# RWKV-7 + FoX trunk on one core: value and bonus rows with the heads of a pair apart, the gate loaded for two chunks at once, the bias row put in order by ScalarE

## The chip, the cores and the metric

The kernel runs on one core of one Trainium2 chip. The metric is the device time of one execution in microseconds (us), lower is better; a kernel's time is the median of several runs.

## The reference

A two-layer decoder trunk in float32: 1024 tokens (T), width 1024 (D), 16 heads of 64. The change lies in the first mixer, RWKV-7 time mixing, of which this is the part that matters:

```python
r, k, v = x_r @ w_rkv[0], x_k @ w_rkv[1], x_v @ w_rkv[2]
g = sigmoid(x_g @ g1) @ g2
def step(S, inp):
    r_t, w_t, k_t, v_t, kk_t, b_t = inp
    sa = einsum('bhvk,bhk->bhv', S, -kk_t)
    S = S * w_t[:, :, None, :] + sa[..., None] * b_t[:, :, None, :] + v_t[..., None] * k_t[:, :, None, :]
    return S, einsum('bhvk,bhk->bhv', S, r_t)
_, y = lax.scan(step, S0, (r, w, k, v, kk, b))
y = group_norm(y) * lnx_w + lnx_b
bonus = sum(r_h * k_h * r_k, axis=-1, keepdims=True) * v_h
x = x + ((y + bonus) * g) @ w_o
```

After it come a squared-ReLU MLP, the shared keys and values, forgetting attention and a second MLP.

## The kernel before, in words

The scan is done in 16 chunks of 64 tokens (`C` = 64, `c` the chunk). The 16 heads are treated as 8 pairs (`NK` = 8, index `p`), `h` is the head within a pair; `P` is 128. Large products are done in float32 split into a high and a low part (`hi`, `lo`; `whi`, `wlo`), three products for one.

The stages, in the profiled run: projections of k and r to 281 us (L863), the projection of v from 281 to 376 us (`proj_tokens`, L884: 768 matmuls of 128x256), the gate's first product to 399 us, then the chunked recurrence, which overlaps the gate's second product at its start and is over by about 690 us, then the rest of the trunk.

**Values.** `emit_v` takes a finished 256-token, 256-column block of v from PSUM (ScalarE copies it to `tv`, L1059), makes the bonus times v in `vb` (ScalarE at L1065 for the first two column blocks, VectorE at L1067 for the others), adds the bias row `lnb` on VectorE (L1071), and writes `vb` to the DRAM array `d_vb` on SyncE's queue (L1072) and `tv` to `d_v` on ScalarE's queue (L1073). Both arrays have the tokens as rows and the columns in the order of the model (pair, head, value). `bon` holds the bonus factor for each token and head (L1033). `lnb` is loaded by one broadcast DMA (L1055).

**Recurrence.** For each chunk `rec_values` loads `Z`, the values of a chunk (L400): for each head of a pair 64 tokens x 8 pairs x 64 values, that is 512 pieces of 256 bytes. `rec_norm` loads `Vh` from `d_vb` in the same way (L543), and `rec_gate_load` loads 128x8x64 of the gate array `d_g` (L563, 1024 pieces of 256 bytes). The chain of one chunk on TensorE is `pp` (AE times Z; ScalarE copies it to `Ps`, L493), `yp`, `sa` (from Ps; VectorE writes Z, L505), `u` (from Z; VectorE writes the next Z, L519), `yp`. `prepare` for the next chunk lies between (`ap`, `tp`, `op`; results `AE` and `BKt`, `TT` copied by ScalarE at L482). GpSimd scales the state `St` (L524), `KRz` (L471) and the block `B` (L435). The tiles of d_T and d_B that a chunk needs are loaded as `TT`, `BT` and `B`.

**Fill.** W_out's products (`wo`) are put between the steps of a chunk to fill TensorE. Their weights come in pieces: SyncE loads `woraw` (L1200), ScalarE casts it to `woh` (L597), and VectorE (L600) or GpSimd (L602) makes the low part `wol`. The gate's second product `gp` fills the first chunks; ScalarE copies it out (L1265: `xt`, `gs`) and writes `d_g` on its own queue (L1267).

**What sets the order.** A scheduler orders the instructions of each engine from a simulated timeline, except where the program order is pinned; a change in one place therefore moves instructions elsewhere. A queue (SyncE's or ScalarE's) issues its DMAs strictly in this order, and each DMA that these two queues issue takes one of eight completion semaphores in turn, so that it waits for the DMA issued eight places before.

Of the kernel before, what the change touches and what calls it, by code (L numbers as in the profile page):

```python
# [390 lines left out]
LANES = [(slice(0, 32), slice(32, 64)), (slice(64, 96), slice(96, 128))]  # L391


def rec_values(k, c):

    nc = k.nc
    Z = k.rc.tile([P, NK, 2, C], F32, tag="Z", name="Z", bufs=2)
    v = k.d_v[c * C:c * C + C, :].rearrange("t (p h v) -> h t p v", h=2, v=C)
    for h in range(2):
        nc.sync.dma_start(Z[HALF[1 - h], :, h], v[h])  # L400
        if c == 0:
            nc.gpsimd.memset(Z[HALF[h], :, h], 0.0)
    return Z


# [78 lines left out]

def rec_solve(k, s, Z):

    nc, c = k.nc, s["c"]
    pp = k.psC.tile([P, NK, C], F32, tag="psC", name="pp")
    for p in range(NK):
        for h, hs in enumerate(HALF):  # L490
            k.pe.matmul(pp[hs, p], s["AE"][:, p, h, 0, :], Z[:, p, h, :], start=True, stop=True)
    Ps = k.rw.tile([P, NK, C], F32, tag="Ps", name="Ps")
    nc.scalar.copy(Ps, pp)  # L493
    yp = s["yp"] = k.psY.tile([P, NK, C], F32, tag="psY", name="yp")
    if c:
        for p in range(NK):
            for h, hs in enumerate(HALF):
                k.pe.matmul(yp[hs, p], s["KR"][hs, p, 1, :], Z[hs, p, h, :], start=p == 0, stop=False)
    yield
    sa = k.psC.tile([P, NK, C], F32, tag="psC", name="sa")  # L500
    for p in range(NK):
        for h, hs in enumerate(HALF):
            k.pe.matmul(sa[hs, p], s["TT"][:, p, h, :], Ps[:, p], start=True, stop=True)
    for h, hs in enumerate(HALF):
        nc.vector.tensor_tensor(Z[hs, :, h], sa[hs], k.ns2[hs, :, c:c + 1].broadcast_to([64, NK, C]), op=ALU.mult)  # L505


def rec_state(k, s, Z, Zn, St):

    nc, c = k.nc, s["c"]  # L510
    u = k.psC.tile([P, NK, C], F32, tag="psC", name="u")
    for p in range(NK):
        for h, hs in enumerate(HALF):
            k.pe.matmul(u[hs, p], s["BKt"][:, p, hs], Z[:, p, h, :], start=True, stop=True)
    for h, hs in enumerate(HALF):
        if St is None:
            nc.vector.tensor_copy(Zn[hs, :, h], u[hs])
        else:
            nc.vector.tensor_tensor(Zn[hs, :, h], u[hs], St[hs], op=ALU.add)  # L519
    if c == NCH - 2:  # L520
        return None
    Sn = k.rw.tile([P, NK, C], F32, tag="St", name="St")
    for h, hs in enumerate(HALF):
        nc.gpsimd.tensor_tensor(Sn[hs], Zn[hs, :, h], k.sc[hs, :, c:c + 1].broadcast_to([64, NK, C]), op=ALU.mult)  # L524
    return Sn


def rec_out(k, s, Z):
    c = s["c"]
    for p in range(NK):  # L530
        for h, hs in enumerate(HALF):
            k.pe.matmul(s["yp"][hs, p], s["AE"][:, p, h, 1, :], Z[:, p, h, :], start=c == 0 and p == 0,
                        stop=p == NK - 1)


def rec_norm(k, s):

    nc, w, w1, c = k.nc, k.rw, k.rw1, s["c"]
    S3 = [P, NK, C]
    cs = slice(c * C, c * C + C)  # L540
    V = w1.tile(S3, F32, tag="Vh", name="Vh")
# [12 lines left out]
    rsqrt_small(k, w, rs, var, 1.0 / C, 64e-5)
    nc.vector.tensor_tensor(Y, Y, rs.unsqueeze(2).broadcast_to(S3), op=ALU.mult)
    nc.gpsimd.tensor_tensor(Y, Y, k.lnw, op=ALU.mult)
    nc.gpsimd.tensor_tensor(Y, Y, V, op=ALU.add)


def rec_gate_load(k, s):  # L560
    c = s["c"]
    s["g"] = k.rw.tile([P, NK, C], F32, tag="g", name="g")
    k.nc.sync.dma_start(s["g"], k.d_g.rearrange("(p f) t -> f p t", f=P)[:, :, c * C:c * C + C])  # L563
# [14 lines left out]
def stage_recurrence(k, a, tile_of, gates):  # L578
    nc, tc = k.nc, k.tc
    with ExitStack() as ctx:  # L580
# [107 lines left out]
        for c in range(NCH):  # L688
# [179 lines left out]

def proj_tokens(k, bank, xs, w, emit, lo_eng):

    wv = w.rearrange("(k p) e -> p k e", p=P)
    G, B = w.shape[1] // 256, T // 256
    for g in range(G):
        with k.tc.high_priority(offset=PRIO):
            pcs = [load_w(k, wv[:, 4 * q:4 * q + 4, 256 * g:256 * g + 256], [P, 4, 256], lo_eng=lo_eng) for q in range(2)]
        os_ = [bank().rearrange("p (j e) -> p j e", j=2) for _ in range(B)]

        for i, b in [(i, b) for i in range(NK) for b in range(B)] if g in (0, G - 1) else \
                [(i, b) for b in range(B) for i in range(NK)]:
            o, (xh, xl), (wh, wl) = os_[b], xs[i], (t[:, i % 4] for t in pcs[i // 4])  # L880
            for j in range(2):
                ts = slice((2 * b + j) * P, (2 * b + j + 1) * P)
                for n, (x, y) in enumerate(((xh, wh), (xh, wl), (xl, wh))):
                    k.nc.tensor.matmul(o[:, j], x[:, ts], y, start=j == 0 and i == 0 and n == 0,  # L884
                                       stop=j == 1 and i == NK - 1 and n == 2)
            if i == NK - 1:
                emit(g, b, o)
# [78 lines left out]
def stage_mix(k, a, right):  # L966
# [5 lines left out]
    with ExitStack() as ctx, ExitStack() as prep:  # L972
# [57 lines left out]
        krs = []  # L1030

        def bonus(e):
            nc.scalar.copy(k.bon[:, :, 2 * e:2 * e + 2].rearrange("p (g j) h -> p g j h", j=2),  # L1033
                           head_sums(k, krs.pop(0), k.pr))

        def emit_r(e, o):
# [1229 lines left out]
```

## Time and profile before

| what | value |
|---|---|
| median of 3 runs | 2531.66 us (2531.41 to 2534.13) |
| profiled execution, its own time | 2531.5 us |
| span of the profiled execution | 2529.8 us, granted TensorE clock 0.999 |
| TensorE (PE) | 2492.7 us busy, 99% |
| weight load (PEld) | 2093.5 us, 83% |
| VectorE (DVE) | 1798.2 us, 71% |
| ScalarE (ACT) | 1284.4 us, 51% |
| GpSimd (POOL) | 423.9 us, 17% |

The span is the time between the first and the last instruction. An engine's busy time is given with its share of the span; SP is SyncE, `SPq` and `ACTq` are the issues of DMAs on the queues of SyncE and ScalarE. In a row of the timeline the first number is the start in us, the second the duration, and what stands in brackets at the end is how long the engine had been idle before and what ended the wait. L12 is line 12 of the kernel before; the changed kernel's lines are up to 18 higher.

### The profile page before, as it was taken

What the parts mean: (1) busy time and instruction counts of PE and PEld (TensorE: products, weight loads), DVE (VectorE), ACT (ScalarE), POOL (GpSimd) and SP (SyncE); (2) the same over time, 40 slices, a digit from 0 to 9 for tenths busy, and PEclk for the clock granted to TensorE, in tenths of its full rate; (3) what the DMA queues carried; (4) which work ended last, traced back from release to release, by engine and by line L of the source; (5) the groups of instructions that cost most, each with busy time, mean ns of one, the idle gap of its engine ahead of it and who ended that gap; (6) DMA issues with size and microseconds to landing.
All of it is one profiled execution on the core that took longest, in us unless ns stands there. A gap on an engine that the chain in (4) does not pass through costs nothing.

```text
span 2529.8 us, 44520 instructions
## 1 busy us (share of the span) xinstructions
PE 2492.7 (99%) x17505; PEld 2093.5 (83%) x17505; DVE 1798.2 (71%) x2892; ACT 1284.4 (51%) x2235; POOL 423.9 (17%) x350
## 2 busy tenths in 40 slices
PE   8999998999999999999999999999999999999999
PEld 5887896788888888888888999888888888878887
DVE  8578895878687777477669576788628777656765
ACT  7682554333464545343456444788526455443332
POOL 2000014645300000003001222355200000000210
PEclk9999999999999999999999999999999999999999
DMA  4668849877344544866741324575223545386664
GB/s 134 149 149 212 235 146 243 204 170 160 79 150 143 173 145 148 288 240 224 237 143 51 119 68 141 152 176 143 95 98 120 184 138 172 122 288 233 225 205 137
DMA packets 415910, 419.88 MB, mean 166 GB/s; under 512 B 189002, under 2 KB 301090, under 8 KB 415700
## 3 DMA queue, kind: packets, MB, share of 16 engines
q1 hardware_dynamic: 401124, 385.69, 51.9%
q0 software_dynamic: 5744, 18.69, 1.9%
q10 hardware_dynamic: 8832, 12.65, 1.5%
q8 instruction: 138, 2.26, 0.4%
q14 instruction: 72, 0.59, 0.1%
HBM read 293.02 MB, written 123.92 MB: 165 GB/s over the span
## 4 chain that ended last, share of the span: by engine, by line
PE 91%; DVE 4%; ACT 2%; issue 1%; DMA 1%; SPq 0%; POOL 0%; ACTq 0%; DVEq 0%; POOLq 0%
PE mm L383 42%; PE mm L794 7%; PE mm L795 7%; PE mm L793 7%; PE mm L863 7%; PE mm L884 4%; PE tp L386 4%; PE wo L383 3%; PE s L383 2%; PE o L383 2%; PE yp L383 1%; PE ap L383 1%; PE z1p L383 1%; DVE l L1981 1%; PE sa L383 1%
## 5 line engine op out<-in xcount | busy, mean ns | idle before, releaser
L383 PE MATMUL mm<-ol,oh 128*128 128x512 f32 x896 | 346.7, 389 | 1.0 <-DVE ol L1593 1.0
L383 PE MATMUL mm<-oh 128*128 128x512 f32 x896 | 346.8, 389 | 0.4 <-ACT oh L1591 0.4
L383 PE MATMUL mm<-oh,ol 128*128 128x512 f32 x896 | 346.6, 389 | 0.0
L757 ACT CAST oh<-ra 128x1024 fp32r<-128x1024 f32 x108 | 113.8, 1054 | 331.1 <-PE mm L383 233.1
L760 DVE TENSOR_TENSOR ol<-ra,oh 128x1024 fp32r<-128x1024 f32 x108 | 137.9, 1276 | 129.4 <-ACT oh L757 129.3
L383 PEld LDWEIGHTS mm<-ol,oh 128*128 128x128 f32 x896 | 168.1, 188 | 36.0 <-DVE ol L1593 1.4
L383 PEld LDWEIGHTS mm<-oh 128*128 128x128 f32 x896 | 168.1, 188 | 35.6 <-ACT oh L1591 0.8
L383 PEld LDWEIGHTS mm<-oh,ol 128*128 128x128 f32 x896 | 168.2, 188 | 35.2
L793 PE MATMUL mm<-xhT,ah 128*128 128x512 f32 x448 | 174.3, 389 | 0.0
L794 PE MATMUL mm<-xlT,ah 128*128 128x512 f32 x448 | 174.3, 389 | 0.0
L795 PE MATMUL mm<-xhT,al 128*128 128x512 f32 x448 | 174.3, 389 | 0.0
L1652 POOL DMA_DIRECT2D xt<-d_xh x8 | 4.4, 549 | 754.8 <-DMA ra<-d_H 418.7
L793 PE MATMUL mm<-xhB,ah 128*128 128x512 f32 x336 | 130.7, 389 | 0.0
L794 PE MATMUL mm<-xlB,ah 128*128 128x512 f32 x336 | 130.7, 389 | 0.0
L795 PE MATMUL mm<-xhB,al 128*128 128x512 f32 x336 | 130.7, 389 | 0.0
L1409 ACT ACTIVATE z<-z 128x512 f32<-128x512 f32 x112 | 70.8, 633 | 108.6 <-DVE z L1406 108.0
L760 DVE TENSOR_TENSOR ol<-rb,oh 128x1024 fp32r<-128x1024 f32 x92 | 120.8, 1313 | 0.2
L757 ACT CAST ah<-w 128x512 fp32r<-128x512 f32 x128 | 79.0, 618 | 79.8 <-PE mm L794 71.2
L1984 ACT ACTIVATE l<-l,mx 128x512 f32<-128x512 f32 (+7 forms) x128 | 99.4, 778 | 26.4 <-DVE mx L1981 25.4
L793 PEld LDWEIGHTS mm<-xhT,ah 128*128 128x128 f32 x448 | 84.1, 188 | 17.6
L795 PEld LDWEIGHTS mm<-xhT,al 128*128 128x128 f32 x448 | 84.1, 188 | 17.4
L794 PEld LDWEIGHTS mm<-xlT,ah 128*128 128x128 f32 x448 | 84.1, 188 | 17.4
(500 smaller groups left out, 6789.4 us busy)
## 6 DMA issues: line engine op xcount, KB each, us to landing
rb<-in_mlp_w_out_dram SPq DMA_DIRECT2D x124, 512.0 KB, 5.6
ra<-d_H SPq DMA_DIRECT2D x108, 512.0 KB, 4.1
w<-in_mlp_w_in_dram SPq DMA_DIRECT2D x64, 512.0 KB, 5.4
d_H<-z SPq DMA_DIRECT2D x56, 512.0 KB, 3.8
d_H<-sums SPq DMA_DIRECT2D x32, 768.0 KB, 5.9
raw<-in_rwkv_w_rkv_dram SPq DMA_DIRECT2D x24, 512.0 KB, 4.7
KRz<-d_KR SPq DMA_DIRECT2D x16, 512.0 KB, 4.8
KRz<-d_BK SPq DMA_DIRECT2D x16, 512.0 KB, 5.7
```

What stands on the lines that cost most here:

```text
L383: return self.tc.keep_in_program_order(self.tc.nc.tensor.matmul(*args, **kw))
L386: return self.tc.keep_in_program_order(self.tc.nc.tensor.transpose(*args))
L757: nc.scalar.copy(hi, src)
L760: lo_eng.tensor_tensor(lo, src, hi.bitcast(F32), op=ALU.subtract)
L793: te.matmul(out, ah, bh, start=i == 0, stop=False)
L794: te.matmul(out, ah, bl, start=False, stop=False)
L795: te.matmul(out, al, bh, start=False, stop=i == n - 1)
L863: nc.tensor.matmul(o[e][half], wt[:, i % 4, es], xs[i][part][:, 512 * half:512 * half + 512], start=i == 0 and wt is hi and part == 0, sto ...
L884: k.nc.tensor.matmul(o[:, j], x[:, ts], y, start=j == 0 and i == 0 and n == 0, stop=j == 1 and i == NK - 1 and n == 2)
L1409: nc.scalar.activation(x, x if o is None else o, AF.Relu)
L1981: nc.vector.tensor_tensor_reduce(l[:, :n0], s[:, :n0], bias[j][:, :n0], -1.0, m, ALU.add, ALU.min, mx[:, 1:2])
L1984: nc.scalar.activation(l, l, AF.Exp, bias=m, scale=-1.0, accum_out=SM[:, j, qb:qb + 1])
```

## The change

1. `d_v` and `d_vb` are laid out anew. Columns: first all even heads, then all odd heads (head, pair, value), so that one head's 8x64 values of a token are 2 KB in one piece. Rows: the two 128-token tiles of a 256-token block in turn (block, token, tile). `chunk_values` gives the rows of a chunk. `Z` becomes [128, 2, 8, 64]. A load of Z or Vh is then 64 pieces of 2 KB where it was 512 of 256 bytes; a write in `emit_v` is 512 pieces of 512 bytes where it was 256 of 1 KB.
2. So that `tv` already has this order, `proj_tokens` reads its moving operand (256 columns of the weights) permuted, in four runs of 64; the PSUM side stays in one piece. `bon` is written with a stride of two.
3. `lnb` is loaded into a scratch tile `lr` and put in the new order by two ScalarE copies of 128x4x128. The load stands later in SyncE's queue: among the last loads of the receptance instead of in the middle of the key stage.
4. The gate is loaded once for two chunks (512-byte pieces, one tile instead of two buffers), and the load stands behind `gate(prev)`, which uses the tile's earlier content.

```diff
+def chunk_values(dv, c):
+    v = dv.rearrange("(b t j) (h p v) -> b j h t p v", j=2, t=P, h=2, v=C)[c // 4, c // 2 % 2]
+    return v[:, C * (c % 2):C * (c % 2) + C]
...
-    Z = k.rc.tile([P, NK, 2, C], F32, tag="Z", name="Z", bufs=2)
-    v = k.d_v[c * C:c * C + C, :].rearrange("t (p h v) -> h t p v", h=2, v=C)
+    Z = k.rc.tile([P, 2, NK, C], F32, tag="Z", name="Z", bufs=2)
+    v = chunk_values(k.d_v, c)
...
-    V = w1.tile(S3, F32, tag="Vh", name="Vh")
+    V, v = w1.tile(S3, F32, tag="Vh", name="Vh"), chunk_values(k.d_vb, c)
     for h in range(2):
-        nc.sync.dma_start(V[64 * h:64 * h + 64], k.d_vb[cs, :].rearrange("t (p h v) -> h t p v", h=2, v=C)[h])
+        nc.sync.dma_start(V[64 * h:64 * h + 64], v[h])
...
-    s["g"] = k.rw.tile([P, NK, C], F32, tag="g", name="g")
-    k.nc.sync.dma_start(s["g"], k.d_g.rearrange("(p f) t -> f p t", f=P)[:, :, c * C:c * C + C])
+    if c % 2 == 0:
+        k.g2 = k.rw1.tile([P, NK, 2, C], F32, tag="g", name="g")
+        k.nc.sync.dma_start(k.g2, k.d_g.rearrange("(p f) (c t) -> f p c t", f=P, t=C)[:, :, c:c + 2])
+    s["g"] = k.g2[:, :, c % 2]
...
-            rec_gate_load(k, cur)
             if prev is not None:
                 gate(prev)
+            rec_gate_load(k, cur)
...
-                    k.nc.tensor.matmul(o[:, j], x[:, ts], y, start=j == 0 and i == 0 and n == 0,
+                    y = y.rearrange("p (q h v) -> p h q v", h=2, v=N)
+                    k.nc.tensor.matmul(o[:, j].rearrange("p (h q v) -> p h q v", h=2, v=N), x[:, ts], y, start=j == 0 and i == 0 and n == 0,
...
-        lnb = k.pi.tile([P, D], F32, name="lnb")
-        nc.sync.dma_start(lnb, a["rwkv_lnx_b"].broadcast_to([P, D]))
+        lnb, lr = k.pi.tile([P, D], F32, name="lnb"), tp_.tile([P, D], F32, tag="o", name="lr", bufs=3)
+        nc.sync.dma_start(lr, a["rwkv_lnx_b"].broadcast_to([P, D]))
+        for h in range(2):
+            nc.scalar.copy(lnb.rearrange("p (g h e) -> p h g e", h=2, g=4)[:, h].rearrange("p g (q v) -> p g q v", v=N),
+                                  lr.rearrange("p (g q h v) -> p h g q v", g=4, q=2, h=2)[:, h])
...
-            nc.sync.dma_start(k.d_vb[256 * b:256 * b + 256, 256 * g:256 * g + 256].rearrange("(j t) e -> t j e", t=P), vb)
-            nc.scalar.dma_start(k.d_v[256 * b:256 * b + 256, 256 * g:256 * g + 256].rearrange("(j t) e -> t j e", t=P), tv)
+            for q, (dv, t) in zip((nc.sync, nc.scalar), ((k.d_vb, vb), (k.d_v, tv))):
+                dv = dv.rearrange("(b t j) (h e) -> b t (j h) e", j=2, t=P, h=2)[b, :, :, P * g:P * g + P]
+                q.dma_start(dv, t.rearrange("p j (h e) -> p (j h) e", h=2))
```

The change also moves instructions. On TensorE the order is the same from the projection of v on; on the other engines it differs at the gate and in the first chunks.

ScalarE, while the first chunk waits for a W_out weight; `woh` is the cast of that weight, `gs` a copy of the gate's product, `TT` four copies of the solve's blocks and `Ps` what TensorE waits for next. Before:

```order
L465 COPY O_4492<-op 128x128
L1265 COPY gs<-gp 128x512
L597 CAST woh_4462<-woraw 128x1024
L482 COPY TT_4332<-op_4518 32x4x32 x2
L1267 DMA d_g<-gs 128x2x512
L482 COPY TT_4332<-op_4518 32x4x32 x2
L493 COPY Ps<-pp 128x512
```

The same place in the changed kernel:

```order
L471 COPY O_4495<-op 128x128
L605 CAST woh_4465<-woraw 128x1024
L1282 COPY gs<-gp 128x512
L488 COPY TT_4335<-op_4521 32x4x32 x4
L1284 DMA d_g<-gs 128x2x512
L499 COPY Ps<-pp 128x512
```

The copy `gs` moved behind the cast, and the write of `d_g` behind the last TT copy.

VectorE, at the end of the projection of v; `lo` is the low part of the gate's two last input blocks, `vb` the bonus rows, `sg` the gate's sigmoid. Before:

```order
L1067 TENSOR_TENSOR vb<-tv,bon 128x512 x2
L992 SCALAR_TENSOR_TENSOR t<-hT_124,c_mug,t 128x1024
L1071 TENSOR_TENSOR vb<-vb,lnb 128x512 x2
L760 TENSOR_TENSOR lo<-t,hi 128x1024 x2
L1067 TENSOR_TENSOR vb<-tv,bon 128x512
L1243 TENSOR_SCALAR sg<-sg 128x512
```

The same place in the changed kernel:

```order
L1083 TENSOR_TENSOR vb<-tv,bon 128x512
L1003 SCALAR_TENSOR_TENSOR t<-hT_124,c_mug,t 128x1024
L1087 TENSOR_TENSOR vb<-vb,lnb 128x512
L768 TENSOR_TENSOR lo<-t,hi 128x1024
L1083 TENSOR_TENSOR vb<-tv,bon 128x512
L768 TENSOR_TENSOR lo<-t,hi 128x1024
L1087 TENSOR_TENSOR vb<-vb,lnb 128x512
```

A bonus product now stands between the two low parts.

GpSimd, from the second to the third chunk; `St` is the scaled state in two halves, `KRz` the scaled keys, `wol` the low part of a W_out weight. Before:

```order
L557 TENSOR_TENSOR Y<-Y,Vh 128x512
L524 TENSOR_TENSOR St<-Z,sc 64x512 x2
L471 TENSOR_TENSOR KRz_4331<-KRz_4331,sc 64x8x64 x2
L602 TENSOR_TENSOR wol_4836<-woraw,woh_4835 128x1024
L435 TENSOR_TENSOR B_5026<-B_5026,ns_89 32x256 x2
```

The same place in the changed kernel:

```order
L530 TENSOR_TENSOR St<-Z,sc 64x512
L610 TENSOR_TENSOR wol_4839<-woraw,woh_4838 128x1024
L530 TENSOR_TENSOR St<-Z,sc 64x512
L477 TENSOR_TENSOR KRz_4334<-KRz_4334,sc 64x8x64 x2
```

The low part moved ahead of the second half of the state and of the keys.

More of the change, by code (lines that the diff above doesn't have):

```diff
@@ L391 @@
 LANES = [(slice(0, 32), slice(32, 64)), (slice(64, 96), slice(96, 128))]
+def chunk_values(dv, c):
+    v = dv.rearrange("(b t j) (h p v) -> b j h t p v", j=2, t=P, h=2, v=C)[c // 4, c // 2 % 2]
+    return v[:, C * (c % 2):C * (c % 2) + C]
 def rec_values(k, c):
     nc = k.nc
-    Z = k.rc.tile([P, NK, 2, C], F32, tag="Z", name="Z", bufs=2)
-    v = k.d_v[c * C:c * C + C, :].rearrange("t (p h v) -> h t p v", h=2, v=C)
+    Z = k.rc.tile([P, 2, NK, C], F32, tag="Z", name="Z", bufs=2)
+    v = chunk_values(k.d_v, c)
     for h in range(2):
-        nc.sync.dma_start(Z[HALF[1 - h], :, h], v[h])
+        nc.sync.dma_start(Z[HALF[1 - h], h], v[h])
         if c == 0:
-            nc.gpsimd.memset(Z[HALF[h], :, h], 0.0)
+            nc.gpsimd.memset(Z[HALF[h], h], 0.0)
     return Z
@@ L490, in rec_solve @@
         for h, hs in enumerate(HALF):
-            k.pe.matmul(pp[hs, p], s["AE"][:, p, h, 0, :], Z[:, p, h, :], start=True, stop=True)
+            k.pe.matmul(pp[hs, p], s["AE"][:, p, h, 0, :], Z[:, h, p, :], start=True, stop=True)
     Ps = k.rw.tile([P, NK, C], F32, tag="Ps", name="Ps")
@@ L497, in rec_solve @@
             for h, hs in enumerate(HALF):
-                k.pe.matmul(yp[hs, p], s["KR"][hs, p, 1, :], Z[hs, p, h, :], start=p == 0, stop=False)
+                k.pe.matmul(yp[hs, p], s["KR"][hs, p, 1, :], Z[hs, h, p, :], start=p == 0, stop=False)
     yield
@@ L504, in rec_solve @@
     for h, hs in enumerate(HALF):
-        nc.vector.tensor_tensor(Z[hs, :, h], sa[hs], k.ns2[hs, :, c:c + 1].broadcast_to([64, NK, C]), op=ALU.mult)
+        nc.vector.tensor_tensor(Z[hs, h], sa[hs], k.ns2[hs, :, c:c + 1].broadcast_to([64, NK, C]), op=ALU.mult)
 def rec_state(k, s, Z, Zn, St):
@@ L513, in rec_state @@
         for h, hs in enumerate(HALF):
-            k.pe.matmul(u[hs, p], s["BKt"][:, p, hs], Z[:, p, h, :], start=True, stop=True)
+            k.pe.matmul(u[hs, p], s["BKt"][:, p, hs], Z[:, h, p, :], start=True, stop=True)
     for h, hs in enumerate(HALF):
         if St is None:
-            nc.vector.tensor_copy(Zn[hs, :, h], u[hs])
+            nc.vector.tensor_copy(Zn[hs, h], u[hs])
         else:
-            nc.vector.tensor_tensor(Zn[hs, :, h], u[hs], St[hs], op=ALU.add)
+            nc.vector.tensor_tensor(Zn[hs, h], u[hs], St[hs], op=ALU.add)
     if c == NCH - 2:
@@ L523, in rec_state @@
     for h, hs in enumerate(HALF):
-        nc.gpsimd.tensor_tensor(Sn[hs], Zn[hs, :, h], k.sc[hs, :, c:c + 1].broadcast_to([64, NK, C]), op=ALU.mult)
+        nc.gpsimd.tensor_tensor(Sn[hs], Zn[hs, h], k.sc[hs, :, c:c + 1].broadcast_to([64, NK, C]), op=ALU.mult)
     return Sn
@@ L531, in rec_out @@
         for h, hs in enumerate(HALF):
-            k.pe.matmul(s["yp"][hs, p], s["AE"][:, p, h, 1, :], Z[:, p, h, :], start=c == 0 and p == 0,
+            k.pe.matmul(s["yp"][hs, p], s["AE"][:, p, h, 1, :], Z[:, h, p, :], start=c == 0 and p == 0,
                         stop=p == NK - 1)
@@ L539, in rec_norm @@
     S3 = [P, NK, C]
-    cs = slice(c * C, c * C + C)
-    V = w1.tile(S3, F32, tag="Vh", name="Vh")
+    V, v = w1.tile(S3, F32, tag="Vh", name="Vh"), chunk_values(k.d_vb, c)
     for h in range(2):
-        nc.sync.dma_start(V[64 * h:64 * h + 64], k.d_vb[cs, :].rearrange("t (p h v) -> h t p v", h=2, v=C)[h])
+        nc.sync.dma_start(V[64 * h:64 * h + 64], v[h])
     yp = s["yp"]
@@ L1032, in bonus @@
         def bonus(e):
-            nc.scalar.copy(k.bon[:, :, 2 * e:2 * e + 2].rearrange("p (g j) h -> p g j h", j=2),
+            s0 = 4 * (e // 2) + e % 2
+            nc.scalar.copy(k.bon[:, :, s0:s0 + 3:2].rearrange("p (g j) h -> p g j h", j=2),
                            head_sums(k, krs.pop(0), k.pr))
```

## The prediction

> **What bounds the kernel now.** I read the page first, then the windows of the stages that the change touches, then TensorE's waits in them, and last the timelines around each wait. The page's first row and the chain:
>
> ```profile
> PE 2492.7 (99%) x17505; PEld 2093.5 (83%) x17505; DVE 1798.2 (71%) x2892; ACT 1284.4 (51%) x2235; POOL 423.9 (17%) x350
> ...
> PE 91%; DVE 4%; ACT 2%; issue 1%; DMA 1%; SPq 0%; POOL 0%; ACTq 0%; DVEq 0%; POOLq 0%
> ```
>
> TensorE is busy for 2492.7 of 2529.8 us, so the whole kernel has some 37 us to give unless TensorE's own work changes. The stages of the change, with the busy time of each engine, the granted clock, the DMA share and GB/s at the end of a row:
>
> ```profile
> 281.00:376.00 95.00, 95.00 (x799) 93.33 (x798) 80.06 (x114) 52.78 (x116) 13.91 (x13) 1.00 0.55 172
> ...
> 395.00:432.00 37.00, 30.73 (x404) 23.60 (x402) 13.44 (x19) 19.11 (x33) 15.19 (x11) 0.95 0.87 212
> 432.00:480.00 48.00, 42.20 (x837) 35.37 (x837) 42.19 (x66) 20.09 (x46) 33.28 (x28) 0.96 0.97 230
> 480.00:545.00 65.00, 65.00 (x1173) 53.42 (x1172) 48.99 (x85) 20.97 (x52) 32.60 (x32) 1.00 0.75 173
> ```
>
> The projection of v (first row) and the chunks in their steady pace (last row) have no TensorE idle: 95.00 of 95.00 and 65.00 of 65.00. All that can be won lies in the first three to four chunks, where DMA is at 0.87 and 0.97: 6.27 and 5.80 us idle, 12.1 us together. What TensorE waits for from 395 to 480 us, in us in total, times, longest:
>
> ```profile
> PE sa L383 <- ACT Ps L493: 5.5, 3, 4.0
> PE u L383 <- DVE Z L505: 1.8, 3, 1.2
> PE pp L383 <- DVE AE L471: 1.6, 2, 1.1
> PE op L383 <- DVE AE L445: 1.0, 3, 0.4
> PE gp L383 <- ACT gs L1265: 0.9, 1, 0.9
> PE yp L383 <- POOL KRz L471: 0.7, 1, 0.7
> ```
>
> No row names Z, Vh or g as a load: the transfers that the change makes cheaper end no wait of TensorE directly. They can count only through what shares the DMA engines with them, or an engine's order.
>
> **Loads of Z and Vh, the steady chunks.** How much DMA do they take? The DMA view of 480 to 545 us (four chunks), and the GB/s row of the densest stage before, 376 to 395 us:
>
> ```profile
> DMA packets 23114, 11.27 MB, mean 173 GB/s; under 512 B 21408, under 2 KB 21408, under 8 KB 23100
> ...
> GB/s 60 397 414 233 0 65 330 408 379 401 293 379 401 371 414 414 414 287 354 347 330 351 343 241 220 209 319 328 259 371 371 295 360 371 265 172 330 181 354 242
> ```
>
> The four chunks keep the DMA engines busy 0.75 x 65 = 48.8 us. At the 414 GB/s that large packets reach, 11.27 MB would take 27.2 us; the other 21.6 us over 21408 small packets are about 1.0 ns each. A chunk's Z, Vh and g are 3072 pieces of 256 bytes, after the change 256 of 2 KB and, per chunk, 512 of 512 bytes: 2304 fewer, an estimate of 2.3 us of 12.2 per chunk. In the steady chunks this lies under a TensorE without idle: worth nothing there, even if it were twice as much. Were that cover gone, it would be at most 2.3 us for each chunk that waits for a DMA.
>
> The page "DMA: Bandwidth & Descriptors" of the Trainium skill (Why small descriptors are slow) gives a fixed 3 cycles beside 8 for a 256-byte descriptor. By it 256 KB at 414 GB/s would take 0.87 us instead of 0.63, so the term that follows here would be -0.2 instead of -0.5; the 1.0 ns for each small packet, some 16 ns on one of the 16 engines against 10 ns for its bytes, is well above that, though 128-byte pieces are in it.
>
> **The long wait of the first chunk.** Its chain, from SyncE's queue over ScalarE to TensorE:
>
> ```profile
> 408.68 1.19 SPq L400 DMA_DIRECT2D Z<-d_v  x2
> 410.03 2.66 SPq L1200 DMA_DIRECT2D woraw<-in_rwkv_w_o_dram  x4
> ```
>
> ```profile
> 414.28 0.59 ACT L1265 COPY gs<-gp 128x512 f32<-128x512 f32 x1 [0.76 <-PE gp L383]
> 417.64 1.04 ACT L597 CAST woh<-woraw 128x1024 fp32r<-128x1024 f32 x1 [2.78 <-DMA woraw<-in_rwkv_w_o_dram]
> 417.77 0.37 ACTq L1267 DMA_DIRECT2D d_g<-gs  x1
> 418.59 1.06 ACT L482 COPY TT<-op 32x128 f32<-32x128 f32 x4
> 419.68 0.59 ACT L493 COPY Ps<-pp 128x512 f32<-128x512 f32 x1
> ```
>
> ```profile
> 420.31 2.04 PE L383 MATMUL sa<-Ps,TT 128*64 128x64 f32 x32 [4.02 <-ACT Ps L493]
> ```
>
> ScalarE stands 2.78 us at a cast whose weight is late, and what TensorE needs, Ps, is queued behind it. The weight was issued at 410.03 right after Z of the second chunk, whose 1024 pieces become 128: by the estimate 0.9 us less DMA ahead of it. Between 0 (the weight shares the engines with other loads) and 0.9 I take -0.5. Against it the copy `gs`, which now fits into the idle time ahead of the cast (414.28), stands behind the cast in the new order and in front of TT: between 0 and its 0.59 us, taken +0.5, since the wait leaves no other cover. The two nearly cancel.
>
> **The second chunk.** ScalarE's order, and TensorE's two rows that depend on it:
>
> ```profile
> 436.67 0.40 ACTq L1267 DMA_DIRECT2D d_g<-gs  x1
> 437.10 0.53 ACT L482 COPY TT<-op 32x128 f32<-32x128 f32 x2 [2.04 <-DMA g<-d_g]
> 437.65 0.59 ACT L493 COPY Ps<-pp 128x512 f32<-128x512 f32 x1
> ```
>
> ```profile
> 436.61 1.00 PE L386 MATMUL tp<-ident,KRz 128*128 128x128 f32 x4
> 438.29 1.15 PE L383 MATMUL sa<-Ps,TT 128*64 128x64 f32 x32 [0.67 <-ACT Ps L493]
> ```
>
> The write of d_g waited 2.04 us for the second load of g, because a DMA takes one of eight completion semaphores in turn. With one load for two chunks that second load is gone, and the write waits for a small TT load issued before it. TensorE gains at most the 0.67 us that it waited, since `tp` ends at 437.6 whatever ScalarE does: between 0 and -0.67, taken -0.65.
>
> **GpSimd between the second and third chunk.** The rows of before, with what waits for them:
>
> ```profile
> 446.26 2.87 POOL L471 TENSOR_TENSOR KRz<-KRz,sc 64x512 f32<-64x512 f32 x2
> 449.21 2.36 POOL L602 TENSOR_TENSOR wol<-woraw,woh 128x1024 fp32r<-128x1024 f32 x1
> ```
>
> ```profile
> 449.54 1.15 PE L383 MATMUL yp<-Z,KRz 64*64 64x64 f32 x32
> ...
> 452.06 1.15 PE L383 MATMUL sa<-Ps,TT 128*64 128x64 f32 x32 [0.79 <-ACT Ps L493]
> ```
>
> ```profile
> 455.34 1.40 DVE L505 TENSOR_TENSOR Z<-sa,ns 64x512 f32<-64x512 f32 x2
> ```
>
> `wol` now goes first, so KRz is ready at 446.26 + 2.36 + 2.87 = 451.5 instead of 449.1, and `yp` waits about 2.0 us. `sa` behind it then starts at about 453.5 to 453.9 instead of 452.06. But VectorE takes `sa`'s result only at 455.34, in its own order, while `sa` ended at 453.2: 2.1 us of slack. So most of the delay is absorbed: between 0 and 1.2, taken +0.3.
>
> **The gate's low parts.** VectorE, then TensorE's product that needs the last of them:
>
> ```profile
> 384.07 2.35 DVE L760 TENSOR_TENSOR lo<-t,hi 128x1024 fp32r<-128x1024 f32 x2
> 387.20 0.87 DVE L1067 TENSOR_TENSOR vb<-tv,bon 128x512 f32<-128x512 f32 x1 [0.78 <-DMA d_vb<-vb]
> ```
>
> ```profile
> 386.83 0.39 PE L383 MATMUL mm<-lo,whi 128*128 128x512 f32 x1
> ```
>
> The last `lo` ended at 386.42, 0.41 us before TensorE came to it. A bonus product of 0.6 to 0.9 us now stands in front of it, and that product waited 0.78 us for the write of its buffer. So TensorE waits between 0.2 and 1.2 us; taken +0.5, near the lower end, as the buffer's write is issued earlier in the new order.
>
> **The projection of v.** TensorE reads the same 256 columns, in four runs of 64:
>
> ```profile
> L884 PE MATMUL mm<-whi,hi x256: 278/283/364, 281.2 to 376.1; 128*128 128x256 f32 x128
> ```
>
> ```profile
> 448.46 1.15 PE L383 MATMUL pp<-Z,AE 128*64 128x64 f32 x32
> ```
>
> 768 matmuls in 95 us are 124 ns each. No row shows a permuted operand. Bounds: nothing, or that four runs cost as much as four matmuls of 64 columns: `pp` has 32 of them in 1.08 us (448.46 to 449.54), 34 ns each, so 135 ns, 11 ns more, 768 x 11 ns = 8.6 us. A gain is excluded: the same columns and products are left. I take 0, nearer to the row of 124 ns, since each run has 64 elements in a row and PSUM is still written in one piece.
>
> The page "Advanced Engine Details and Errata" of the Trainium skill (PSUM Cachelines) says that any non-contiguous pattern slows matmuls significantly, and that every two consecutive elements should be contiguous; read by its first half the projection gets longer, by its second it stays.
>
> **The rest, each at nothing.** The writes of `emit_v` carry the same bytes at a DMA share of 0.55. The two copies into `lnb` (two of about 0.6 us, as `gs` above) fit in ScalarE's idle time before the first `tv`:
>
> ```profile
> 305.70 0.17 ACT L1033 COPY bon<-sums 128x16 f32<-128x16 f32 x1 [2.71 <-PE sums L217]
> ```
>
> Behind the later load of the bias stand writes and one weight load, all used tens of us later; without this cover the load costs what it takes to land. The load of g stands now behind VectorE's use of the old tile, with the loads of BT, x and Vh queued behind it on SyncE. In the steady pace that use is over before SyncE comes to the load:
>
> ```profile
> 498.34 0.41 SPq L563 DMA_DIRECT2D g<-d_g  x1
> ```
>
> ```profile
> L573 DVE TENSOR_TENSOR z<-zp,g x2: 683/683/683, 496.1 to 511.6; 128x512 f32<-128x512 f32 x2
> ```
>
> 496.1 + 0.7 = 496.8, 1.5 us ahead; were it gone, BT would come late by the difference, and `op` with it.
>
> **The sum.** -0.5 +0.5 -0.65 +0.3 +0.5 +0 = +0.15 us on the profiled execution's own 2531.5, which lies 0.2 us under the median of 2531.66. I forecast 2531.8 us: no change. From the ends of the terms: -0.9 -0.67 +0.2 = -1.4 to +0.59 +1.2 +1.2 = +3.0 without the projection, 2530.1 to 2534.5. About 0.2%, 5.1 us, is what a measurement of this kernel can tell from no change.
>
> **The rivals.** (A) The crowded start eases. If the lighter Z and the single g bring the late weights forward by some 3 us, the three waits for Ps fall from 5.5 to about 1.0 us, `sa` after the long one runs in 1.15 instead of 2.04 us (TensorE had run slower after the idle time), and the small waits lose some 0.6: -6.0, 2525.5 us. For it speaks the DMA share of 0.87 and 0.97; against it that the weight's issue follows GpSimd's release of its buffer, and that the pieces saved ahead of it are worth 0.9 us. It decides from 2.5 us on.
>
> (B) The permuted operand slows the projection: +8.6 us, 2540.3 us. TensorE is there without idle, so every ns counts 768 times; it is slower than before from 6.6 ns a matmul on. Against it speaks the length of the runs.
>
> (C) New waits, in one place: the start. The orders of GpSimd, VectorE and ScalarE cost their upper ends, +3.0, and each of the three waits is followed by slow matmuls as the one at 420.31 was (0.9 us each): +5.7, 2537.3 us. Against it speaks the slack of 2.1 us before Z.
>
> **How the numbers follow.** Forecast 0.60, A 0.21, B 0.08, C 0.11. The range of 8 in 10 takes in A and C and leaves out B and the outer tails: 2525.2 to 2537.5 us. Faster by over 0.2% is A, 0.21; slower B and C, 0.19; within 0.2% the forecast, 0.60.
>
> **What would show it.** Right: the steady chunks have 65.00 of 65.00 again with a lower DMA share; the wait for Ps near 420 us stays between 3.5 and 4.5 us; the one near 438 is gone; a wait of `yp` for KRz near 450 is new; the group of L884 still takes 95 us. Wrong: L884's matmuls more than some ns longer (B), a wait for Ps of under 2 us (A), or TensorE idle in the steady chunks.

## The result, and the profile after

The changed kernel took 2536.40 us (median of 20 runs), the kernel before 2533.97 us (median of 20 runs taken with it): a ratio of 1.0014, 95% interval 1.0007 to 1.0020. Measured twice more it was 1.0005 (0.9997 to 1.0014) and 1.0011 (1.0002 to 1.0020). Each ratio is taken over the fast runs and leaves out single slow ones (one of 3630.51 us before, one of 5142.48 us after); the two medians alone would give 1.0010. So the change costs some 0.10%, about 2.5 us (the mean of the three): less than the 0.2% below which the forecast saw no change, but two of the three intervals lie above 1. The kernel is slightly slower where the forecast said that the terms cancel.

The page of the changed kernel, engines and chain:

```profile
PE 2500.7 (98%) x17505; PEld 2099.7 (83%) x17505; DVE 1796.8 (71%) x2892; ACT 1284.7 (51%) x2237; POOL 422.7 (17%) x350
...
PE 90%; DVE 4%; DMA 2%; ACT 2%; issue 2%; SPq 0%; POOL 0%; ACTq 0%; DVEq 0%; POOLq 0%
```

TensorE still bounds the kernel. Its busy time rose by 8 us in this execution, with the same 17505 matmuls: they ran at a lower granted clock (0.995 against 0.999 over the whole span). The windows:

```profile
281.00:376.00 95.00, 95.00 (x778) 92.13 (x778) 79.87 (x116) 50.49 (x117) 11.21 (x12) 1.00 0.64 190
395.00:432.00 37.00, 31.93 (x330) 23.81 (x330) 11.65 (x19) 19.33 (x34) 10.45 (x8) 0.95 0.83 212
432.00:480.00 48.00, 40.30 (x788) 33.62 (x784) 39.97 (x58) 20.64 (x46) 33.08 (x27) 0.89 0.86 235
480.00:545.00 65.00, 65.00 (x1196) 53.50 (x1190) 47.43 (x86) 20.34 (x51) 33.09 (x33) 1.00 0.66 181
```

The steady chunks have no idle, as before; their DMA share fell from 0.75 to 0.66. The DMA view of that window shows why, and that this was worth nothing:

```profile
DMA packets 14314, 11.79 MB, mean 181 GB/s; under 512 B 9367, under 2 KB 11415, under 8 KB 14302
```

The small packets fell from 21408 to 9367. The permuted operand of the projection of v:

```profile
L895 PE MATMUL mm<-whi,hi x256: 278/284/384, 284.7 to 380.4; 128*128 128x256 f32 x128
```

284 ns where it was 283, and the group lasts from 284.7 to 380.4, 95.7 us; before, 281.2 to 376.1, 94.9. The difference is not the operand: late_bias_early, an experiment below that has the permuted operand but the order of before, has this row:

```profile
L895 PE MATMUL mm<-whi,hi x256: 278/283/364, 280.4 to 375.3; 128*128 128x256 f32 x128
```

That is again 283 ns and 94.9 us. And only_bias_late, which has the old operand and the new order, needs 95.6 us (280.8 to 376.4). What makes the group longer is the order of the head sums at its start, to which the part on the failed step returns. The rest of the stage is equal to 0.03 us in the table below.

What is new are waits of TensorE. From 220 to 300 us:

```profile
PE sums L212 <- DVE kr L315: 1.7, 1, 1.7
```

and from 300 to 500 us:

```profile
PE sa L383 <- ACT Ps L499: 6.0, 2, 3.7
...
PE mm L383 <- DVE lo L768: 0.9, 1, 0.9
```

Of these, the wait for the low part (`lo`) was in the forecast, and of the two waits for Ps the long one, 3.7 us, which stood there before. The other wait for Ps, 2.3 us, was not, since that one was to go away. Nor was the wait of `sums`: `sums` are the head sums of the bonus (the product of r, k and r_k summed over a head), four small matmuls in the middle of the projection of r, 80 us before any row of v is written.

**Where the time went, over all profiles.** One execution is not enough here: the profiled one of the changed kernel took 2543.2 us, the two others 2532.1 and 2532.7. TensorE has 17505 matmul records in each kernel, so the time between the same two records can be set beside each other. The table does this for five stages, in us (named by their time in the first profile of before), for 17 profiles; the kernels are those of the experiments below.

| kernel | ratio | 35 to 308 | 308 to 376 | 376 to 406 | 406 to 515 | 652 to 1798 |
|---|---|---|---|---|---|---|
| before | | 272.67 | 68.40 | 29.35 | 109.43 | 1145.96 |
| before_again | 1.0004 | 271.17 | 68.40 | 29.41 | 111.17 | 1149.59 |
| only_gate_two | 1.0001 | 271.64 | 68.40 | 29.38 | 113.01 | 1146.01 |
| late_bias_early | 0.9998 | 271.98 | 68.40 | 29.37 | 111.86 | 1146.04 |
| late_bias_early_2 | 0.9994 | 271.17 | 68.40 | 29.39 | 108.15 | 1145.98 |
| only_layout | 1.0005 | 271.20 | 68.40 | 29.37 | 111.43 | 1150.93 |
| bias_early_write_pool | 0.9994 | 271.23 | 68.40 | 29.35 | 110.41 | 1152.47 |
| late_load_unused | 1.0008 | 271.78 | 68.40 | 29.68 | 113.10 | 1146.34 |
| late_and_spare | 1.0027 | 272.03 | 68.40 | 29.81 | 111.70 | 1150.01 |
| late_and_spare_2 | 1.0021 | 271.62 | 68.40 | 29.66 | 111.34 | 1151.14 |
| only_bias_late | 1.0013 | 272.96 | 68.37 | 29.31 | 109.90 | 1146.54 |
| changed_gate_single | 1.0013 | 273.19 | 68.37 | 29.66 | 110.33 | 1146.89 |
| changed | 1.0014 | 275.29 | 68.37 | 30.23 | 112.50 | 1149.54 |
| changed_again | 1.0005 | 273.71 | 68.37 | 29.11 | 108.53 | 1146.72 |
| changed_third | 1.0011 | 273.32 | 68.37 | 29.67 | 109.49 | 1145.92 |
| no_bias | 1.0005 | 273.12 | 68.40 | 29.10 | 112.50 | 1148.66 |
| gate_write_pool | 1.0014 | 273.42 | 68.37 | 29.11 | 109.71 | 1146.44 |

The first ten kernels have TensorE's order of before through the projection of r, the last seven the order of the changed kernel. In the first stage the two groups do not overlap: 271.17 to 272.67, mean 271.65, against 272.96 to 275.29, mean 273.57. That is 1.9 us. The last two columns move by 3.6 to 6.5 us within each group (the last one by 3.6 us between the two profiles of the kernel before), and this is most of the spread between these profiles.

### The profile page after: what moved, and what is told of

It is laid out like the page before. It is cut to its first block, busy times and chain, and to the rows that moved or that the text cites. A ratio compares the mean times of both kernels' runs of the same rounds, so it can differ in the third digit from the quotient of the medians.

```text
span 2541.4 us, 44501 instructions
## 1 busy us (share of the span) xinstructions
PE 2500.7 (98%) x17505; PEld 2099.7 (83%) x17505; DVE 1796.8 (71%) x2892; ACT 1284.7 (51%) x2237; POOL 422.7 (17%) x350
## 4 chain that ended last, share of the span: by engine, by line
PE 90%; DVE 4%; DMA 2%; ACT 2%; issue 2%; SPq 0%; POOL 0%; ACTq 0%; DVEq 0%; POOLq 0%
PE mm L383 41%; PE mm L801 7%; PE mm L802 7%; PE mm L803 7%; PE mm L871 6%; PE tp L386 4%; PE wo L383 3%; PE mm L895 3%; PE s L383 2%; PE o L383 2%; PE z1p L383 1%; PE ap L383 1%; PE yp L383 1%; PE sa L383 1%; DVE l L1998 1%
## 5 line engine op out<-in xcount | busy, mean ns | idle before, releaser
L768 DVE TENSOR_TENSOR al<-w,ah 128x512 fp32r<-128x512 f32 x128 | 87.7, 686 | 16.9 <-ACT ah L765 14.4
```

What stands on the lines that cost most here:

```text
L768: lo_eng.tensor_tensor(lo, src, hi.bitcast(F32), op=ALU.subtract)
```

## The experiments

Theory 1: the moved load of the bias row is the cause. In 1a it costs because the scheduler re-orders the projection of r; in 1c because a load at the late place costs by itself; 1b stands for 1c or the wait for the gate's low part. Theory 2: the gate's doubled load makes the TT blocks of the second chunk late. Theory 3: chance. In the code cuts `...` stands for lines left out.

### The parts apart

**late_bias_early**: the changed kernel, with the scratch tile in a space of its own instead of the space of r's tiles; the load then goes out early.

```diff
-        lnb, lr = k.pi.tile([P, D], F32, name="lnb"), tp_.tile([P, D], F32, tag="o", name="lr", bufs=3)
+        lnb, lr = k.pi.tile([P, D], F32, name="lnb"), k.pi.tile([P, D], F32, name="lr")
```

> The changed kernel with one edit: the bias row's scratch tile has its own space, so its load stands again where it stood before the change (TensorE and VectorE then have the order of before). Theory 1 (the moved bias load re-ordered the projections and the gate's low parts): the 1.7 us wait of the head sums for kr near 228 us and the 0.9 us wait for the last low part near 391 us are gone, and the time is 2.7 us below the changed kernel, about 1.0003 of before. Theory 2 (the doubled gate load delays the TT blocks of the second chunk): no difference to the changed kernel, 1.0014 of before, and the wait of sa for Ps of 2.3 us in the second chunk stays.

Measured: 0.9998 of before (0.9989 to 1.0007), as theory 1 expected. In its profile the wait of the sums for kr is shorter but not gone (0.7 us), and `sa` still waits 1.9 us for Ps in the second chunk: that wait is there without the cost that theory 2 put on it.

**only_bias_late**: the kernel before, with the bias row alone as in the change.

```diff
-        nc.sync.dma_start(lnb, a["rwkv_lnx_b"].broadcast_to([P, D]))
+        lr = tp_.tile([P, D], F32, tag="o", name="lr", bufs=3)
+        nc.sync.dma_start(lr, a["rwkv_lnx_b"].broadcast_to([P, D]))
+        for h in range(2):
+            nc.scalar.copy(lnb[:, 512 * h:512 * h + 512], lr[:, 512 * h:512 * h + 512])
```

> The kernel before with one part of the change: the bias row loaded into the scratch tile and copied (in the old column order) by ScalarE, so that its load moves to the late place. Theory 1: the waits of 1.7 us (head sums for kr) and 0.9 us (low part) appear, 1.0011 of before. Theory 2: 1.0000 of before, no new wait of TensorE over 0.5 us in the second chunk.

Measured: 1.0013 (1.0004 to 1.0023). TensorE's wait from 220 to 300 us:

```profile
PE sums L212 <- DVE kr L315: 1.0, 1, 1.0
```

The expected wait for the low part did not come in this execution (376 to 406 us: 29.31).

**only_gate_two**: the kernel before with the gate's load of the change.

```diff
+    if c % 2 == 0:
+        k.g2 = k.rw1.tile([P, NK, 2, C], F32, tag="g", name="g")
...
-            rec_gate_load(k, cur)
             if prev is not None:
                 gate(prev)
+            rec_gate_load(k, cur)
```

> The kernel before with one part of the change: the gate loaded for two chunks at once behind the use of the old tile. Theory 1: 1.0000 of before. Theory 2: the first doubled load, ahead of the TT blocks on the queue, makes them late; ScalarE's write of d_g waits for one of them, Ps behind it, TensorE waits over 2 us for Ps in the second chunk and runs slowly after it: 1.0012 of before, +3 us.

Measured: 1.0001 (0.9993 to 1.0010). Theory 2 is not borne out in the time; in the second chunk `sa` waited 0.5 us for Ps, not 2.

**changed_gate_single**: the changed kernel with the gate's load of before (the last diff the other way round).

> The changed kernel with the gate loaded for one chunk at a time as before. Theory 1: the waits in the projections stay, 1.0011 of before. Theory 2: the wait for Ps in the second chunk falls to 0.7 us or less, 3 us below the changed kernel, 1.0002 of before.

Measured: 1.0013 (1.0004 to 1.0021). Undoing the gate's load gives nothing back.

**only_layout**: both undone, late_bias_early with the gate's load of before.

> The changed kernel with the bias row loaded at the old place and the gate loaded for one chunk at a time: the new rows of values and bonus and the permuted operand alone. Theory 1a: 1.0000 of before, 35 to 308 us in under 272.5 us. Theory 2 (the two-chunk gate load makes the start of the recurrence longer): no wait of sa for Ps over 1 us in the second chunk, 406 to 515 us of before in under 111 us.

Measured: 1.0005 (0.9995 to 1.0016); in the profile 271.20 for the first stage and 111.43 for 406 to 515 us (expected under 111). In the second chunk `sa` waited 1.2 us for Ps although the gate is loaded singly, against theory 2 again.

Of the first four, the two with the late load cost 0.13%, the two without it nothing. The first stage shows how, in one execution of each kind. The changed kernel (changed_again), TensorE, with VectorE's product that it waits for:

```profile
226.77 0.39 PE L871 MATMUL mm<-hi,wlo 128*128 128x512 f32 x1
228.83 0.63 PE L212 MATMUL sums<-kr,heads 128*32 128x256 f32 x4 [1.68 <-DVE kr L315]
```

```profile
225.94 0.69 DVE L314 TENSOR_TENSOR Er<-r,Er 128x512 f32<-128x512 f32 x1 [1.17 <-DMA Er<-d_E]
...
227.98 0.75 DVE L315 SCALAR_TENSOR_TENSOR kr<-Er,cols,kr 128x512 f32<-128x512 f32 x1 [0.19 <-DMA kr<-d_BK]
```

The same place with the load at its old place (late_bias_early_2):

```profile
228.75 0.61 PE L871 MATMUL mm<-hi,whi 128*128 128x512 f32 x2
229.30 0.63 PE L212 MATMUL sums<-kr,heads 128*32 128x256 f32 x4
```

```profile
228.11 0.75 DVE L315 SCALAR_TENSOR_TENSOR kr<-Er,cols,kr 128x512 f32<-128x512 f32 x1
```

VectorE's product ends at 228.7 in one and 228.9 in the other: kr is ready at nearly the same time. TensorE comes to the sums at 227.2 in the first, after 9 matmuls fewer, and at 229.3 in the second. That the bias load's old place decides this order is shown by late_and_spare and no_bias below. The likely way, which no run shows since the scheduler's timeline was not recorded: with the bias load gone from SyncE's queue ahead of the loads of Er and kr, that timeline has them earlier and puts the sums earlier. On the chip they are hardly earlier; the issues of Er, changed_again and then late_bias_early_2:

```profile
222.87 0.40 SPq L301 DMA_DIRECT2D Er<-d_E  x1
```

```profile
223.21 0.38 SPq L301 DMA_DIRECT2D Er<-d_E  x1
```

0.3 us, while the sums moved by 2.1.

### The order, or the load itself

**late_and_spare**: the changed kernel with a second load of the row at the old place in the queue, used by nothing; the order of the projection of r is then that of before, the bias still comes late.

```diff
+        spare = k.pi.tile([P, D], F32, name="spare")
+        nc.sync.dma_start(spare, a["rwkv_lnx_b"].broadcast_to([P, D]))
         nc.sync.dma_start(lr, a["rwkv_lnx_b"].broadcast_to([P, D]))
```

> The changed kernel, the bias row still loaded at the late place, with a second load of the same row, used by nothing, at the old place in the queue. With it the scheduler gives TensorE the order of before through the projection of r (head sums later again); a bonus row still stands between the gate's two last low parts. Theory 1a (the cost is the order of the projection of r: head sums put ahead of their data): no wait of the sums for kr over 0.8 us, 1.0001 of before. Theory 1b (the cost is the late load itself or the low part): 1.0013 of before, as the changed kernel.

Measured: 1.0027 (1.0018 to 1.0036), slower than anything else. Neither theory foresaw that. The first stage came out as 1a says, 272.03, and the wait near 228 us was

```profile
PE sums L212 <- DVE kr L315: 0.8, 1, 0.8
```

so the time is lost elsewhere.

**no_bias**: the changed kernel with zeros for the bias row, which is left out of the computation: no load at either place, the order of the changed kernel.

```diff
...
-        nc.sync.dma_start(lr, a["rwkv_lnx_b"].broadcast_to([P, D]))
...
+        nc.gpsimd.memset(lnb, 0.0)
```

> The changed kernel without the bias row: it is left out of the computation (zeros instead), so there is no load of it at either place and no copy. TensorE's order in the projection of r is that of the changed kernel. Theory 1a: a wait of the sums for kr of over 1 us near 228 us, and 1.0010 to 1.0014 of before though nothing is loaded late. Theory 1b: 1.0000 to 1.0003 of before if the load is the cost, 1.0004 if the low part is.

Measured: 1.0005 (0.9996 to 1.0014), below the 1.0010 to 1.0014 that 1a expected and above the figures of 1b, and too wide to decide between them. The wait for kr was 1.2 us and the first stage 273.12, though nothing is loaded late: the order alone makes the stage longer.

**changed_again** and **before_again**: the two kernels once more.

> The changed kernel once more, for a second profile. Theories 1a and 1b: 1.0014 of before, with the wait of the sums for kr over 1 us again. If the extra 1.8 us at 10 to 75 us and 3.6 us near 1775 us of its first profile belong to the change, they are here again; if they are a matter of single executions, at most one of them is.

> The kernel before once more, against itself: 1.0000, and the width of its interval is what the other ratios have to exceed. All theories: no wait of the sums for kr over 0.8 us between 220 and 260 us; its wait for r of 1.0 us near 217 us and its first-chunk wait of 4.0 us show how far single waits move between two executions.

Measured: 1.0005 (0.9997 to 1.0014) and 1.0004 (0.9995 to 1.0013). The interval of a kernel against itself reaches 0.13%, so no single ratio here settles a theory; the groups and the stages do. The 1.8 us at the start and the 3.6 us near 1775 us of the first profile were not there in the second one of the changed kernel. The latter came in the second of before: chance, as far as the change goes.

**late_bias_early_2**: that kernel again.

> The kernel late_bias_early once more, for a second profile. Theory 1a: below 1.0006 of before, 35 to 308 us in under 272.5 us (early order) where the changed kernel needs over 273. Theory 2: ScalarE's write of d_g waits again over 2 us for a TT load in the second chunk and sa waits for Ps over 1 us.

Measured: 0.9994 (0.9985 to 1.0002); 271.17 in the first stage. The two figures of this kernel, 0.9998 and 0.9994, are below all three of the changed one. Theory 2 fails here too: ScalarE stood 0.35 us at its write of d_g, not over 2 us, and `sa` waited 0.5 us.

**gate_write_pool** and **bias_early_write_pool**: the changed kernel and late_bias_early, each with the second half of the gate's writes on GpSimd's queue.

```diff
-                    nc.scalar.dma_start(k.d_g[(e - 1) * P:(e + 1) * P, s].rearrange("(b p) t -> p b t", p=P), t)
+                    (nc.gpsimd if half else nc.scalar).dma_start(k.d_g[(e - 1) * P:(e + 1) * P, s].rearrange("(b p) t -> p b t", p=P), t)
```

> The changed kernel with the second half of the gate's writes on GpSimd's queue, which has completion semaphores of its own, so that ScalarE no longer waits there for a TT load. Theory 2: the wait of sa for Ps in the second chunk is gone (under 0.7 us), 406 to 515 us in 110 us or less, 1.0006 of before, where the changed kernel has 1.0005 to 1.0014. Theory 1a: the cost of the projection of r stays, 273 us or more for 35 to 308 us.

> Both repairs: the bias row loaded at the old place, and the second half of the gate's writes on GpSimd's queue. If theories 1a and 2 hold together, 0.9990 to 0.9998 of before: 35 to 308 us in under 272.5 us and 406 to 515 us in 110 us or less. If neither is the cause, 1.0010.

Measured: 1.0014 (1.0005 to 1.0023) and 0.9994 (0.9985 to 1.0002). The second chunk's wait for Ps is gone in both, 406 to 515 us took 109.71 and 110.41, and the time did not move against the same kernel without this edit (theory 2 expected 1.0006 for the first): changed 1.0014, 1.0005, 1.0011, late_bias_early 0.9998, 0.9994. Theory 2 is refuted as a cause of the whole; theory 1 holds, since the early bias, which undoes the order and the late load together, again takes the 0.1% away.

**late_and_spare_2**, **late_load_unused** and **changed_third**. The second is late_bias_early with a second, unused load at the late place:

```diff
         nc.sync.dma_start(lr, a["rwkv_lnx_b"].broadcast_to([P, D]))
+        spare = tp_.tile([P, D], F32, tag="o", name="spare", bufs=3)
+        nc.sync.dma_start(spare, a["rwkv_lnx_b"].broadcast_to([P, D]))
```

> The kernel late_and_spare once more. Theory 1c (a load of the bias row at the late place costs by itself, beside the order): again 1.002 or more of before, with 35 to 308 us under 272.5 us and the loss elsewhere. Theory 3 (the odd figure came from chance stalls, such as a VectorE product in the attention stage that stands still while GpSimd works): nearer to 1.0005.

> The kernel late_bias_early (bias row from the load at the old place) with a second load of the row at the late place, used by nothing: TensorE's order through the projection of r is that of before. Theory 1c: 1.0010 or more of before. Theory 1a: 1.0000 to 1.0005 (a bonus row stands between the two last low parts again, worth up to 0.5 us).

> The changed kernel a third time. Theory 1a: 1.0005 to 1.0014 of before, the wait of the sums for kr over 1 us again, 35 to 308 us in over 273 us.

Measured: 1.0021 (1.0013 to 1.0030), 1.0008 (1.0000 to 1.0017) and 1.0011 (1.0002 to 1.0020). late_and_spare costs as much again, with a short first stage (271.62) and 1151.14 in the last column: that is what 1c expected, and not what theory 3 did. Its waits from 1600 to 1830 us:

```profile
PE s L383 <- DVE mx L2000: 4.0, 3, 2.2
```

This is the stall described under the hardware below. Both profiles of this kernel have it, and neither of late_bias_early; why it meets this stall more often than others is not shown. Nor is it shown that the stall is the whole of it: the fastest of its 23 executions took 2534.17 us, 3.3 us above the fastest of before in the same series. late_load_unused lies between the bounds of 1a and 1c.

By the times alone, then, the late load is as good a cause as the order: the three figures with the late load and the early order are 1.0008 to 1.0027, the one with the late order and no load is 1.0005. That the order costs 1.9 us rests on the first stage, where the groups do not overlap; what the late load costs by itself, if anything, shows in no stage of the table, beyond some 0.3 us from 376 to 406 us in these three.

## Why the prediction was right or wrong

**The size and the sign.** 2531.8 us with no change was forecast, from terms that summed to +0.15 us. The change cost about 2.5 us. The median of before, too, was 2532.7 to 2534.5 in the later series, not 2531.66; three runs had given the low end of its spread.

**The step that failed** is the one that called "the rest, each at nothing": "Behind the later load of the bias stand writes and one weight load, all used tens of us later". That looked only at who waits for what is behind the load at its new place. It should have looked at what stood behind it at its old place: the loads of Er and kr, and, because a scheduler presumably places TensorE's sums by them, the order of the projection of r. The moved order was there to be seen ahead of time, and it was given no term. It measured +1.9 us (271.65 to 273.57); the stage had no slack, since TensorE was busy there for 79.98 of 81 us before.

Set between the same records, these 1.9 us lie in two places. About 1.3 us lie from 227 to 236 us of before, where the seven kernels with the late order wait 1.0 to 1.7 us for kr and the others 0 to 0.8. In the first profile of the changed kernel the matmuls behind this wait also ran slower (granted clock 0.82 from 228 to 233 us, 1.00 in changed_again behind the same wait), so that its 275.29 is the longest. The other 0.7 us lie from 301 to 308 us and contain no wait. There, at the start of the projection of v, the eight last head sums stand together before:

```profile
301.86 0.64 PE L212 MATMUL sums<-kr,heads 128*32 128x256 f32 x8
```

and in two groups in changed_again:

```profile
302.26 0.62 PE L212 MATMUL sums<-kr,heads 128*32 128x256 f32 x4
...
305.76 0.62 PE L212 MATMUL sums<-kr,heads 128*32 128x256 f32 x4
```

A group of four takes as long as one of eight, so a second group costs its whole time. The stretch took 7.57 us in each of the ten profiles and 8.29 in each of the seven. So the sentence ahead of the prediction, that TensorE's order is the same from the projection of v on, holds only from 309 us on: these sums stand inside that projection.

**The loads of Z, Vh and g** were forecast at nothing in the steady chunks: right (65.00 of 65.00, and 1.0001 to 1.0005 for their parts alone). The DMA engines were busy there for 0.66 x 65 = 42.9 us instead of 48.8, about 1.5 us less for each chunk where 2.3 was estimated.

**The projection of v** was forecast at nothing between 0 and +8.6: right, 68.40 to 68.37 in the table. Rival B is out. The page "Advanced Engine Details and Errata" of the Trainium skill (PSUM Cachelines) says that any non-contiguous pattern slows matmuls significantly, and that pairs of elements should stay adjacent. The trace agrees with the second half; the first half it does not bear out for the moving operand: that is read in four runs, with pairs adjacent and the PSUM side in one piece, and a matmul takes 283 ns as before.

**The gate's low part** was forecast at +0.5 between 0.2 and 1.2: 30.23, 29.11 and 29.67 in the changed kernel's profiles against 29.35 to 29.41, +0.3 on the mean. A small term, rightly made, though in the second of the three profiles the wait did not come.

**The long wait of the first chunk** was forecast at nothing net: right, 3.7, 4.3 and 4.0 us in the changed kernel's three profiles, against 4.0 and 2.9 in the two of before. Rival A is out, as the wait did not shrink. The two terms of half a microsecond that were to cancel are smaller than this spread, and no run tells them apart.

**The second chunk** was forecast at -0.65, the wait near 438 us gone: wrong in mechanism. ScalarE, in the changed kernel:

```profile
443.42 0.39 ACTq L1284 DMA_DIRECT2D d_g<-gs  x1
443.85 0.52 ACT L488 COPY TT<-op 32x128 f32<-32x128 f32 x2 [3.92 <-DMA TT<-d_T]
444.39 0.58 ACT L499 COPY Ps<-pp 128x512 f32<-128x512 f32 x1
```

and TensorE:

```profile
445.03 1.98 PE L383 MATMUL sa<-Ps,TT 128*64 128x64 f32 x32 [2.28 <-ACT Ps L499]
446.94 2.08 PE L383 MATMUL ap<-KRz 64*128 64x128 f32 x16
```

The write's place in the turn of the eight semaphores fell on a TT load, as was said, but that load was taken to be quick because it is small. The times from issue to landing of these TT loads, in the first profile of before and of the changed kernel:

```profile
DMA to landing us min/median/max: 6.2/6.5/6.7
```

```profile
DMA to landing us min/median/max: 9.2/9.2/9.3
```

32 KB behind g and KRz on the same queue are not quick: the medians are 6.5 and 7.4 us behind 1.25 MB in the two profiles of before, and 9.2, 6.9 and 7.9 us behind 1.5 MB in the three of the changed kernel. The wait of `sa` varied: 2.3 us, none and 1.3 us in these three, and 0.7 and 1.9 us before, where the write waited for g. Over the start (406 to 515 us) the changed kernel has 112.50, 108.53 and 109.49, before 109.43 and 111.17: no cost on the mean.

**GpSimd's order** was forecast at +0.3 with a wait of `yp` for KRz of about 2.0 us. A wait came, but of 0.65 us, followed by one for Z:

```profile
459.33 1.14 PE L383 MATMUL yp<-Z,KRz 64*64 64x64 f32 x30 [0.65 <-POOL KRz L477]
...
464.75 1.15 PE L383 MATMUL u<-Z,BKt 128*64 128x64 f32 x30 [0.40 <-DVE Z L511]
```

The wait of `sa` for Ps (0.79 us) and one of `u` for Z (1.17 us), which stood there in the first profile of before, are gone. Between the same records, 448.2 to 457.1 us of the first profile of before, the stretch took 8.4, 8.6 and 7.9 us in the changed kernel's profiles against 8.9 and 8.3: no cost. The term was small, as forecast, but the wait that it was made from was taken three times too long.

**Rival C** put the new waits at the start of the recurrence, 5.7 us in sum. A new wait was part of the cause, but the one that counts stood some 170 us earlier.

**What stays open.** 1.9 us of the order and 0.3 us of the low part make 2.2 of some 2.5 us; the rest is below what these runs resolve. That the late load costs something by itself is not excluded, and the figure of late_and_spare is explained only as far as its two profiles show the stall. No version beat the kernel before clearly: late_bias_early (0.9998 and 0.9994) and bias_early_write_pool (0.9994) are the lowest, some 0.15% below the changed kernel, and their intervals reach 1.

## What to carry to other kernels

Where a scheduler sets the order, a moved transfer is priced at its old place too: list what stood behind it there, and which engine's instructions are placed by those arrivals. Of an order that has changed, every place on the engine without idle time gets a term, also those far from the edited code. Where the effect is near 0.1%, compare stages between the same two records over several profiles, and run the kernel against itself.

## What the runs showed of the hardware

A VectorE product with two operands in SBUF stood still while GpSimd worked on a product of its own. In the attention stage, before_again, VectorE and then GpSimd:

```profile
1771.37 3.39 DVE L2087 TENSOR_TENSOR Q<-raw,Q 64x1024 fp32r<-64x1024 f32 x1
```

```profile
1771.30 2.38 POOL L2029 TENSOR_TENSOR o<-o,R 128x1024 f32<-128x1024 f32 x1 [4.36 <-DMA R<-d_sm]
```

and in the first profile of before, where VectorE came first:

```profile
1771.51 1.22 DVE L2087 TENSOR_TENSOR Q<-raw,Q 64x1024 fp32r<-64x1024 f32 x1
```

```profile
1771.83 3.15 POOL L2029 TENSOR_TENSOR o<-o,R 128x1024 f32<-128x1024 f32 x1 [4.78 <-DMA R<-d_sm]
```

The engine that starts first keeps the way: 3.39 us instead of 1.22 when GpSimd was 0.07 us ahead. Wherever VectorE started first in the 17 profiles, if only by 0.01 us, it kept its 1.22 us. TensorE then waits and runs slowly afterwards, and the whole costs about 3.6 us (1149.59 against 1145.96 in the table's last column). Eight of the 17 profiles have such a product of over 2.3 us. GpSimd's product waits for a transfer (R), so that some 0.1 us in its landing decides; that looks like chance, but why some kernels have it more often is open. The page "GPSIMD Engine Reference" of the Trainium skill (Specifications) says that GpSimd's way into SBUF is shared with VectorE for instructions with two SBUF inputs; the traces agree.

In the second chunk of the first profile of the changed kernel TensorE's matmuls took nearly twice as long for some 10 us (granted clock 0.50 from 440 to 445 us and 0.53 from 445 to 450): `sa` and `ap` 1.98 and 2.08 us behind the wait of 2.3 us, against 1.15 and 1.16 elsewhere. That wait did not bring it about, since `yp` at 439 us, ahead of it, took 1.86 us against 1.15 already; ahead of that stood only waits of up to 1.14 us. In late_bias_early `sa` took 1.22 us right behind a wait of 3.35 us. So how long a wait makes the matmuls behind it slow is not settled by these runs.
